# Loads of the attention heads issued from the SyncE queue in place of ScalarE's

## The chip, the cores and the metric

The kernel runs on one core of one Trainium2 chip. The metric is the device time of one launch in microseconds (us), the median of three runs; lower is better. Engines are named as in the profile: PE is the matrix engine, DVE the vector engine, ACT the scalar engine (ScalarE), POOL GpSimd, and SP the SyncE queue. A DMA is issued by an instruction in the program of SP or ACT, and the profile lists such issues as SPq and ACTq; the bytes then move on 16 DMA engines of the core.

## The reference, cut to what matters

One inference step of a trunk of two layers, in float32, on 640 tokens of width 1024: 512 noisy ("latent") tokens and 128 of a new prompt. In each layer one input projection feeds three groups of heads, whose outputs are put side by side for one output projection; a SwiGLU feed-forward part with a hidden width of 2816 follows, and both halves end in a layer norm with modulated shift, scale and gate.

```python
z = (x * (1 + scale_m) + shift_m) @ w_in          # columns split among A, B and C
o_a = diff_attention(q1, q2, k1, k2, v, lam)      # A: 4 heads, two softmax maps each
o_b, s_d = delta_mixer(...)                       # B: gated DeltaNet, both directions, chunks of 64
o_c, s_h = hgrn_mixer(...)                        # C: HGRN2, both directions, chunks of 16
o = concatenate([o_a, o_b, o_c])                  # then @ w_out, layer norm, feed-forward, layer norm

def diff_attention(...):                          # per block of 128 queries
    s1 = einsum(q1, k1) * scale;  s2 = einsum(q2, k2) * scale
    p = softmax(s1) - lam * softmax(s2)
    return einsum(p, v)
```

Latent queries read the 512 latent keys and 128 cached ones; the prompt's queries read the prompt's keys alone. New keys and values of the prompt, and the final states of B and C, are outputs too.

## The kernel before

Matrix products keep nearly full float32 accuracy by splitting an operand into a high part in the faster fp32r format and a remainder: for each weight tile `raw` that a DMA brings, ACT casts the high half of a tile `hl` (L273) and DVE subtracts to get the low half (L176). Tiles `hl` sit in a ring of four buffers, weight tiles `raw` in one that SP fills (L254).

A layer runs in stages that overlap. The input projection writes the queries and keys of all attention heads to scratch in DRAM (`qkhi` for the high parts, `qksc` for the low parts and the prompt, L1318 and L1319), values to `vsc`, and B's outputs to `osc`. Its last pieces are `ci`/`gt` (PE `pci`, one of five token blocks each) and `cq` (PE `pcq`, two blocks in two halves). Beside these runs the DeltaNet chain: PE steps `pdc`, and for each of five token blocks an output that goes through `do`, `doh` (one buffer) and a gate `gd` that SP loads, and is stored to `osc` by ACT (L1048). Then attention runs head after head beside HGRN (`ph`, `hq`, `hqm`) and the modulation products `psm`, whose weights `w_mod` SP loads.

The attention of a head needs 17 loads, which the change touches. `attn_load_qk` (L1139 to L1173) issues 12 into two buffers of the `hl` ring, the query tile `aqs` and the key tile `aks` (L1151 to L1157), and three of cached keys into `ack` (L1159, L1161), of which there is one buffer; PE then transposes (`pack`), and ACT and DVE put the result behind the latent keys (L1167, L1172). `attn_load` adds two loads of values into `avf` (L1183, L1184). Head 0's first 15 are called in `proj_C` ahead of the two `pcq` blocks (L1293), its values when attention begins (L1382), and those of head h+1 in the middle of head h (L1215). In attention PE computes scores `pas`, DVE their maximum `anm`, ACT the exponentials `ae` (L1131), PE transposes (`pat`, copied by ACT to `apT`) and multiplies by the values (`pao`, copied by ACT to `ao`, L1103).

The order of instructions on every engine is not that of the Python code: the program is built inside a context that simulates a timeline of all engines and places each instruction by it (`schedule_with_timeline_sim=True`, L1767). An engine then runs its own list strictly in that order, so an instruction that waits holds what stands behind it, DMA issues included. Completions of DMAs of both queues share eight semaphores that are taken in turn: a DMA is issued only when the eighth one before it has landed, whichever queue issued that.

Of the kernel before, what the change touches and what calls it, by code (L numbers as in the profile page):

```python
# [10 lines left out]
F32 = mybir.dt.float32  # L11
# [8 lines left out]
P = 128  # L20
D = 1024
DEPTH = 2
NLAT = 512
NPRO = 128
NTOK = NLAT + NPRO
NT = NTOK // P
# [83 lines left out]
def tile_trunk(  # L110
# [52 lines left out]
    def psS(cls, name):  # L163
        ps = ps_next(cls, [P, 512], name)
        return ps[:, 0, :] if len(ps.shape) == 3 else ps
# [4 lines left out]
    V, A, G, S = nc.vector, nc.scalar, nc.gpsimd, nc.sync  # L170
# [4 lines left out]
    def tt(eng, out, a, b, op):  # L175
        return eng.tensor_tensor(out, a, b, op)  # L176
# [276 lines left out]
    vsc = [dr.tile([NTOK, 512], F32, name=f"vsc{l}") for l in range(DEPTH)]  # L453
# [3 lines left out]
    qksc = [dr.tile([2, AH, P, NTOK], F32, name=f"qksc{l}") for l in range(DEPTH)]  # L457
    qkhi = [dr.tile([2, AH, P, NLAT], F32, name=f"qkhi{l}") for l in range(DEPTH)]
# [680 lines left out]
    def attn_load_qk(l, h, cls):  # L1139
        qs = phl.tile([P, 2, 1024], F32R, tag="hl", bufs=4, name="aqs")  # L1140
        ks = phl.tile([P, 2, 1024], F32R, tag="hl", bufs=4, name="aks")
        qd, qp = qs[:, 0].rearrange("p (m t) -> p m t", m=2), qs[:, 1, :P].bitcast(F32)
        kflat = ks.rearrange("p x t -> p (x t)")
        kd = kflat[:, :2 * NTOK].rearrange("p (m t) -> p m t", m=2)
        kl = [kflat[:, 2 * NTOK:3 * NTOK], qs[:, 1, P:P + NTOK]]
        kp = kflat[:, 3 * NTOK:].bitcast(F32)
        lo_ = qksc[l]
        qf_, kf_ = qd.bitcast(F32), kd.bitcast(F32)
        hv = [slice(64 * m, 64 * m + 64) for m in range(2)]
        for m in range(2):  # L1150
            A.dma_start(qf_[hv[m], m], qkhi[l][0, h, hv[m]])  # L1151
            A.dma_start(qf_[hv[1 - m], m], lo_[0, h, hv[m], :NLAT])
            A.dma_start(kf_[hv[m], :, :NLAT], qkhi[l][1, h].rearrange("(m j) t -> j m t", m=2))
            for i in range(2):
                A.dma_start(kl[m].bitcast(F32)[hv[i], :NLAT], lo_[1, h, hv[m], :NLAT])
        A.dma_start(qp, qksc[l][0, h, :, NLAT:])
        A.dma_start(kp, qksc[l][1, h, :, NLAT:])  # L1157
        ck = cp.tile([P, 2, P], F32, tag="ack", bufs=1, name=f"ack{l}_{h}")
        A.dma_start(ck[:, 0], cache_attn_k[0, l, :, h, :])  # L1159
        for m in range(2):  # L1160
            A.dma_start(ck[:, 1, hv[1 - m]], cache_attn_k[0, l, :, h, hv[m]])  # L1161
        ps = psS(cls, f"pack{l}_{h}")
        for m in range(2):
            nc.tensor.transpose(ps[:, m * P:(m + 1) * P], ck[:, m], ident)
        nc.tensor.transpose(ps[:, 2 * P:3 * P], kp, ident)
        ko = cp.tile([P, P], F32, tag="akp", bufs=1, name=f"akp{l}_{h}")
        A.copy(ko, ps[:, 2 * P:3 * P])  # L1167
        A.dma_start(new_attn_k[0, l, :, h, :], ko)
        for m in range(2):
            for i in range(2):  # L1170
                src = ps[hv[i], (i ^ m) * P:((i ^ m) + 1) * P]
                A.copy(kd[hv[i], m, NLAT:], src)  # L1172
                tt(V, kl[m][hv[i], NLAT:], src, kd[hv[i], m, NLAT:].bitcast(F32), ALU.subtract)  # L1173
        return qd, kd, kl, qp, kp
# [3 lines left out]
    def attn_load(l, h, ap_):  # L1178
        n_ = f"{l}_{h}"
        qd, kd, kl, qp, kp = early_qk.pop((l, h), None) or attn_load_qk(l, h, "pt")  # L1180
        vf = ap_.tile([P, NT + 1, P], F32, tag="avf", bufs=2, name=f"avf{n_}")
        hs = slice(h * P, (h + 1) * P)
        A.dma_start(vf[:, :NT], vsc[l][:, hs].rearrange("(t p) v -> p t v", p=P))  # L1183
        A.dma_start(vf[:, NT], cache_attn_v[0, l, :, h, :])  # L1184
        return qd, kd, kl, qp, kp, vf

    def attention(l, h, ap_, got):
        n_ = f"{l}_{h}"
        qd, kd, kl, qp, kp, vf = got.pop(h)
        for qt in range(LT):  # L1190
            nn = f"{n_}_{qt}"
            views = []
            qsl = slice(qt * P, (qt + 1) * P)
            for m in range(2):
                ps = psB("as", f"pas{nn}_{m}")
                for hf in range(2):
                    hsl = slice(hf * 320, (hf + 1) * 320)
                    mm(ps[:, hf, :320], qd[:, m, qsl], kd[:, m, hsl], start=True, stop=False)
                    mm(ps[:, hf, :320], qd[:, m, qsl], kl[m][:, hsl], start=False, stop=True)
                views.append(ps[:, :, :320])  # L1200
            p, ri = softmax_pair(l, views, NTOK, ap_, nn)
            pt = psS("pt", f"pat{nn}").rearrange("p (b t) -> p b t", t=P)
            po = psS("po", f"pao{nn}")
            for kt in range(LT):
                nc.tensor.transpose(pt[:, kt, :], p[:, kt * P:(kt + 1) * P], ident)
            nc.tensor.transpose(po[:, P:2 * P], p[:, LT * P:], ident)
            pT = ap_.tile([P, NT, P], F32, tag="apT", bufs=2, name=f"apT{nn}")
            A.copy(pT[:, :LT], pt)
            A.copy(pT[:, LT], po[:, P:2 * P])
            for kt in range(NT):  # L1210
                mm(po[:, :P], pT[:, kt, :], vf[:, kt if kt < LT else NT],
                   start=(kt == 0), stop=(kt == NT - 1))
            attn_tail(l, h, qt * P, po[:, :P], ri[:, 0:1], ap_, nn)
            if qt == PRE[l] and h + 1 < AH:
                got[h + 1] = attn_load(l, h + 1, ap_)  # L1215
            yield
# [57 lines left out]
    def proj_C(l, xT, wp):  # L1274
        W = w_in[l]
        for i in range(4):
            ps = gemm_T(colunit(W, C_CF + i * P), xT, f"pcf{l}_{i}")
            d_, a_ = i // 2, i % 2
            z = wp.tile([P, NTOK], F32, tag="cb", bufs=2, name=f"cf{l}_{i}")
            evac(z, ps, AF.Sigmoid)  # L1280
            V.tensor_scalar(z, z, lbi[:, l, d_, a_:a_ + 1], lbv[:, l, d_, a_:a_ + 1], ALU.mult, ALU.add)
            S.dma_start(cfs[l][i * P:(i + 1) * P, :], z)
            yield
        us = [(rowunit(W, 2 * i, 2, C_CI, 512), [2 * i, 2 * i + 1]) for i in range(4)]
        for tau in range(NT):
            ps = psS("n", f"pci{l}_{tau}")
            gemm_N(ps, 512, xT, tau, us)
            z = wp.tile([P, 256], F32, tag="ca", bufs=2, name=f"ci{l}_{tau}")
            A.copy(z, ps[:, :256])
            S.dma_start(cis[l][tau * P:(tau + 1) * P, :], z)  # L1290
            gate_out(l, ps[:, 256:512], prm[l]["cn"], tau, 256, wp)
            yield
        early_qk[(l, 0)] = attn_load_qk(l, 0, "d1")  # L1293
        for i in range(2):
            ps = gemm_T(colunit(W, C_CQ + i * P), xT, f"pcq{l}_{i}")
            z = wp.tile([P, NTOK], F32, tag="cb", bufs=2, name=f"cq{l}_{i}")
            evac(z, ps, AF.Silu)
            S.dma_start(cqs[l][i * P:(i + 1) * P, :], z)
            yield
# [45 lines left out]
    for l in range(DEPTH):  # L1345
# [35 lines left out]
        def attn():  # L1381
            got = {0: attn_load(l, 0, tp)}  # L1382
            for h in range(AH):
                yield from attention(l, h, tp, got)
            flush(l, 0)
# [182 lines left out]
        for tau in range(NT):  # L1568
# [4 lines left out]
            j = 0 if tau < LT else 1  # L1573
# [91 lines left out]
        for part, (f0, f1) in enumerate(FF_PARTS):  # L1665
# [39 lines left out]
            for nh, tau in order:  # L1705
                us = usn[nh] if nh in usn else usn.setdefault(nh, out_units(nh))
                cs = slice(nh * 512, (nh + 1) * 512)
                j = 0 if tau < LT else 1
# [62 lines left out]
```

## Time and profile before

| | |
|---|---|
| time, median of 3 runs | 2103.04 us (2100.37 to 2107.04) |
| the profiled execution: its time, its span | 2098.58 us, 2096.8 us |
| busy share PE, PE weight loads | 91%, 80% |
| busy share DVE, ACT, POOL | 69%, 38%, 43% |
| mean granted PE clock | 0.956 of full speed |
| bytes moved, mean rate | 249.36 MB, 119 GB/s |
| DMAs issued in the ACT program | 154: 136 loads of the heads, 10 stores of `osc`, 8 of new keys |

The span runs from the first instruction to the last; the time of that execution is 1.8 us longer. A share of busy time is a mean over unlike stages, so it is read together with the windows: a stage whose PE is busy all the time cannot be shortened by the other engines, a stage with idle PE time can.

### The profile page before, as it was taken

How to read it: one execution, taken by the hardware profiler on the slowest of the kernel's cores; microseconds unless marked ns; L12 is line 12 of the kernel's file. 1: busy time of each engine (PE TensorE's matmuls, PEld its weight loads, DVE VectorE, ACT ScalarE, POOL GpSimd, SP SyncE). 2: the span in 40 equal slices, each digit the busy share in tenths (PEclk: the TensorE clock that was granted, in tenths of full speed). 3: DMA queues.
4: the chain of work that ended last, by engine and by line, in shares of the span. 5: the costliest groups of instructions: out<-in, count | busy, mean ns of one | idle time of the engine just before them, and what ended most of it. 6: DMA issues, size and time to landing. Idle time of an engine off the chain costs nothing. (4 is left out here: it accounts for less than half of the span.)

```text
span 2096.8 us, 37785 instructions
## 1 busy us (share of the span) xinstructions
PE 1915.2 (91%) x14914; PEld 1681.5 (80%) x14914; DVE 1440.6 (69%) x2516; ACT 791.2 (38%) x1564; POOL 891.6 (43%) x988
## 2 busy tenths in 40 slices
PE   7999997778988999999989999977799799999996
PEld 5988986657768899989989979755687779989895
DVE  5458534778588866667666784368857897667676
ACT  3542322647143334333336323135742434334331
POOL 0375234766142132435156924357642411432445
PEclk7999998899999999999999999989889999999998
DMA  9423215872653322222434342377235232223221
GB/s 303 112 74 123 90 64 149 225 221 74 211 181 89 114 81 91 71 81 81 133 94 131 108 135 67 102 186 231 87 130 159 84 111 91 71 81 97 76 76 76
DMA packets 243399, 249.36 MB, mean 119 GB/s; under 512 B 19370, under 2 KB 190358, under 8 KB 243222
## 3 DMA queue, kind: packets, MB, share of 16 engines
q1 hardware_dynamic: 221046, 227.27, 35.0%
q10 hardware_dynamic: 22176, 19.67, 3.6%
q8 instruction: 118, 1.93, 0.4%
q14 instruction: 59, 0.48, 0.1%
HBM read 218.72 MB, written 28.18 MB: 118 GB/s over the span
## 5 line engine op out<-in xcount | busy, mean ns | idle before, releaser
L176 DVE TENSOR_TENSOR hl<-raw,hl 128x1024 fp32r<-128x1024 f32 (+1 forms) x210 | 280.1, 1337 | 88.7 <-ACT hl L273 70.9
L173 PE MATMUL pfo<-hl,ha 128*128 128x512 f32 x1320 | 312.9, 395 | 1.5 <-ACT hl L273 0.8
L173 PEld LDWEIGHTS pfo<-hl,ha 128*128 128x128 f32 x1320 | 246.1, 187 | 60.7 <-DVE ft L176 1.2
L176 POOL TENSOR_TENSOR r<-r,ft 128x512 f32<-128x512 f32 x96 | 143.0, 1510 | 248.4 <-DVE ft L176 247.7
L176 POOL TENSOR_TENSOR t<-raw 128x512 f32<-128x512 f32 x44 | 67.9, 1543 | 338.7 <-DMA raw<-in_w_ffn_in_dram 145.4
L173 PE MATMUL pfa<-xT,hl 128*128 128x320 f32 x1056 | 175.3, 316 | 8.7 <-DVE ms L176 3.5
L273 ACT CAST hl<-raw 128x1024 fp32r<-128x1024 f32 (+2 forms) x122 | 125.5, 1036 | 147.8 <-DMA raw<-in_w_ffn_out_dram 45.9
L173 PE MATMUL pfc<-sx,hl 128*128 128x320 f32 x1056 | 172.2, 311 | 9.4 <-ACT hl L1550 8.2
L173 PEld LDWEIGHTS pfa<-xT,hl 128*128 128x128 f32 x1056 | 162.7, 193 | 12.4 <-ACT sx L1513 3.9
L173 PEld LDWEIGHTS pfc<-sx,hl 128*128 128x128 f32 x1056 | 160.4, 189 | 13.0 <-ACT hl L1550 9.0
L1550 ACT CAST hl<-raw 128x1024 fp32r<-128x1024 f32 x88 | 92.1, 1051 | 207.7 <-PE pfo L173 104.4
L173 PE MATMUL paq<-xT,hl 128*128 128x320 f32 x768 | 123.1, 317 | 0.6 <-ACT az L1238 0.6
L173 PE MATMUL pop<-hl,xT 128*128 128x512 f32 x480 | 118.0, 402 | 0.7 <-ACT ae_p L1131 0.7
L173 PEld LDWEIGHTS paq<-xT,hl 128*128 128x128 f32 x768 | 115.7, 190 | 3.4 <-issue 1.2
L173 PEld LDWEIGHTS pop<-hl,xT 128*128 128x128 f32 x480 | 89.6, 191 | 24.9 <-issue 4.7
L176 POOL TENSOR_TENSOR hK<-hK,hT 64x256 f32<-64x256 f32 x120 | 90.6, 755 | 33.4 <-PE ph L173 27.7
L176 DVE TENSOR_TENSOR ft<-pfo,lg 128x512 f32<-128x512 f32 x96 | 63.8, 683 | 55.5 <-PE pfo L173 44.1
L173 PE MATMUL pfd<-xT,h 128*128 128x320 f32 x528 | 87.7, 316 | 9.9 <-DVE u L176 9.9
L176 DVE TENSOR_TENSOR t<-raw,t 128x512 f32<-128x512 f32 x88 | 73.9, 840 | 33.1 <-POOL t L176 33.0
L173 PE MATMUL pbq<-xT,hl 128*128 128x320 f32 x576 | 89.9, 313 | 1.0 <-DVE hl L176 0.4
L173 PEld LDWEIGHTS pfd<-xT,h 128*128 128x128 f32 x528 | 81.4, 193 | 11.4 <-issue 8.7
L173 PE MATMUL pfb<-sx,hl 128*128 128x320 f32 x528 | 88.6, 310 | 0.6 <-DVE hl L176 0.6
(409 smaller groups left out, 4213.0 us busy)
## 6 DMA issues: line engine op xcount, KB each, us to landing
raw<-in_w_ffn_in_dram SPq DMA_DIRECT2D x96, 512.0 KB
raw<-in_w_mod_dram SPq DMA_DIRECT2D x80, 512.0 KB
raw<-in_w_in_dram SPq DMA_DIRECT2D x56, 512.0 KB
raw<-in_w_ffn_out_dram SPq DMA_DIRECT2D x44, 512.0 KB
pc<-in_w_mod_dram SPq DMA_DIRECT2D x8, 1024.0 KB
raw<-in_w_out_dram SPq DMA_DIRECT2D x16, 512.0 KB
qksc<-az SPq DMA_DIRECT2D x16, 320.0 KB
qkhi<-azs SPq DMA_DIRECT2D x16, 256.0 KB
```

The source lines that it names most:

```text
L173: nc.tensor.matmul(out, lhsT, rhs, start=start, stop=stop, **kw)
L176: return eng.tensor_tensor(out, a, b, op)
L273: A.copy(hl[:, 0, :kt * n], raw[:, :kt * n])
L1550: A.copy(tile_[:, 0, :n], raw)
```

## The change

All 17 loads per head, 136 in the two layers, are issued by SP in place of ACT. Sizes, sources and targets stay as they are. The store of B's output to `osc` (L1048) and that of the new keys (L1168) stay on ACT.

```diff
         for m in range(2):
-            A.dma_start(qf_[hv[m], m], qkhi[l][0, h, hv[m]])
-            A.dma_start(qf_[hv[1 - m], m], lo_[0, h, hv[m], :NLAT])
-            A.dma_start(kf_[hv[m], :, :NLAT], qkhi[l][1, h].rearrange("(m j) t -> j m t", m=2))
+            S.dma_start(qf_[hv[m], m], qkhi[l][0, h, hv[m]])
+            S.dma_start(qf_[hv[1 - m], m], lo_[0, h, hv[m], :NLAT])
+            S.dma_start(kf_[hv[m], :, :NLAT], qkhi[l][1, h].rearrange("(m j) t -> j m t", m=2))
             for i in range(2):
-                A.dma_start(kl[m].bitcast(F32)[hv[i], :NLAT], lo_[1, h, hv[m], :NLAT])
-        A.dma_start(qp, qksc[l][0, h, :, NLAT:])
-        A.dma_start(kp, qksc[l][1, h, :, NLAT:])
+                S.dma_start(kl[m].bitcast(F32)[hv[i], :NLAT], lo_[1, h, hv[m], :NLAT])
+        S.dma_start(qp, qksc[l][0, h, :, NLAT:])
+        S.dma_start(kp, qksc[l][1, h, :, NLAT:])
         ck = cp.tile([P, 2, P], F32, tag="ack", bufs=1, name=f"ack{l}_{h}")
-        A.dma_start(ck[:, 0], cache_attn_k[0, l, :, h, :])
+        S.dma_start(ck[:, 0], cache_attn_k[0, l, :, h, :])
         for m in range(2):
-            A.dma_start(ck[:, 1, hv[1 - m]], cache_attn_k[0, l, :, h, hv[m]])
+            S.dma_start(ck[:, 1, hv[1 - m]], cache_attn_k[0, l, :, h, hv[m]])
...
-        A.dma_start(vf[:, :NT], vsc[l][:, hs].rearrange("(t p) v -> p t v", p=P))
-        A.dma_start(vf[:, NT], cache_attn_v[0, l, :, h, :])
+        S.dma_start(vf[:, :NT], vsc[l][:, hs].rearrange("(t p) v -> p t v", p=P))
+        S.dma_start(vf[:, NT], cache_attn_v[0, l, :, h, :])
```

Since the timeline decides the order, the lists of all five engines change in the mixer stages and a little in the start; ACT's shrinks from 1480 rows to 1356, SP's grows from 357 to 479. In the rows below a minus is a row of before, a plus one of after; names carry the layer and block number.

The first place is on ACT in layer 0, at the end of the projection, where head 0's loads stand: `hl` there are the halves of the weights for `pcq`.

```order
 L958 COPY dvn_4_2896<-pdt_4_2891 128x2x2x64
-L1153 DMA aks<-qkhi_443 64x2x512
-L1155 DMA aks<-qksc_441 64x512 x2
-L1048 DMA osc_429<-doh_1_2803 128x256
-L1153 DMA aks<-qkhi_443 64x2x512
-L1157 DMA aks<-qksc_441 128x128
+L273 CAST hl<-raw 128x1024
 L1289 COPY ci_4_3659<-pci_4_3634 128x256
 L1242 ACTIVATE gt_4_256_3662<-pci_4_3634 128x256
-L273 CAST hl<-raw 128x1024 x2
+L273 CAST hl<-raw 128x1024
+L1048 DMA osc_429<-doh_1_2803 128x256
```

The loads ahead of the casts are gone, and the store of block 1's output moved behind the casts.

The second place is ACT in layer 0 just ahead of the first exponential, whose table load is the last row; the rows with `cq_0` and `cq_1` are the last pieces of the projection.

```order
+L1048 DMA osc_429<-doh_3_3085 128x256
+L1238 ACTIVATE cq_0_3754<-pcq_0_0_1_3729 128x320
 L1238 ACTIVATE cq_1_3813<-pcq_1_0_0_3763 128x320
-L1161 DMA ack_1_3933<-in_cache_attn_k_dram 128x64
-L1172 CAST aks<-pack_0_3684 64x128
-L1048 DMA osc_429<-doh_3_3085 128x256
-L1172 CAST aks<-pack_0_3684 64x128
+L1048 DMA osc_429<-doh_4_3203 128x256
 L1238 ACTIVATE cq_1_3813<-pcq_1_0_1_3788 128x320
-L1183 DMA avf_0_3824<-vsc_433 128x5x128
-L1184 DMA avf_0_3824<-in_cache_attn_v_dram 128x128
 L1131 ACT_TABLE_LOAD
```

The loads left the list here too, but the stores of the last two B blocks (3 and 4) now stand ahead of the last `cq` pieces and so of the first exponential; before, that of block 4 came after the second exponential.

At the same place SP has these rows: the gate load `gd_4`, which block 4's output needs, and the loads of head 1.

```order
+L685 DMA gd_3_3094<-gsc_431 128x256
+L1159 DMA ack_1_3933<-in_cache_attn_k_dram 128x128
+L1161 DMA ack_1_3933<-in_cache_attn_k_dram 128x64 x2
+L1088 DMA out_dram<-dSf_999 64x2x64 x4
+L685 DMA gd_4_3212<-gsc_431 128x256
 L1298 DMA cqs_435<-cq_0_3754 128x640
-L685 DMA gd_3_3094<-gsc_431 128x256
-L685 DMA gd_4_3212<-gsc_431 128x256
-L1088 DMA out_dram<-dSf_999 64x2x64 x4
```

`gd_4` moved behind the `ack` loads of head 1, which need PE's `pack` of head 0, and behind the stores of the final state `dSf`.

The third place is ACT in layer 1, at the end of the projection.

```order
 L958 COPY dvn_4_13187<-pdt_4_13182 128x2x2x64
+L1048 DMA osc_430<-doh_1_13094 128x256
+L273 CAST hl<-raw 128x1024
 L1289 COPY ci_4_13950<-pci_4_13925 128x256
 L1242 ACTIVATE gt_4_256_13953<-pci_4_13925 128x256
 L273 CAST hl<-raw 128x1024
+L967 COPY du_10737<-pdu_4_13196 128x512
+L976 COPY dwT_10738<-pdw_4_13214 128x4x64 x2
 L1238 ACTIVATE cq_0_14045<-pcq_0_0_0_13995 128x320
-L976 COPY dwT_10738<-pdw_4_13214 128x4x64
-L1048 DMA osc_430<-doh_1_13094 128x256
```

Here the store of block 1's output moved ahead of the casts of the weights for `pcq`; before, it came after them and after the first `cq` piece.

## Rows read from the trace of the kernel before

**Rows 1.** The page: busy by engine; DMA queues (q1 SP's, q10 ACT's).

```profile
PE 1915.2 (91%) x14914; PEld 1681.5 (80%) x14914; DVE 1440.6 (69%) x2516; ACT 791.2 (38%) x1564; POOL 891.6 (43%) x988
...
q1 hardware_dynamic: 221046, 227.27, 35.0%
q10 hardware_dynamic: 22176, 19.67, 3.6%
```

**Rows 2.** Windows: stretch, length, busy us (instructions), granted clock, DMA share, GB/s.

```profile
700.00:1000.00 300.00, 298.24 (x1757) 276.14 (x1757) 214.12 (x304) 103.78 (x152) 112.26 (x72) 1.00 0.27 81
300.00:360.00 60.00, 47.76 (x606) 41.04 (x597) 25.57 (x74) 11.44 (x27) 25.38 (x34) 0.94 0.40 116
360.00:450.00 90.00, 68.65 (x738) 49.32 (x738) 66.67 (x145) 45.66 (x139) 61.14 (x107) 0.87 0.84 234
1360.00:1390.00 30.00, 19.24 (x169) 16.38 (x170) 16.55 (x46) 6.80 (x16) 14.29 (x23) 0.78 0.57 145
```

**Rows 3.** Tile `aks`, issues: count, ns min/median/max, first and last start.

```profile
L1155 ACTq DMA_DIRECT2D aks<-qksc x16: 452/582/1272, 316.2 to 1461.0; - x16
```

**Rows 4.** The same for tile `ack`.

```profile
L1161 ACTq DMA_DIRECT2D ack<-in_cache_attn_k_dram x16: 334/360/452, 1.1 to 1471.6; - x16
```

**Rows 5.** Timeline of ACT, layer 0: start, duration, line, what, [idle before, releaser].

```profile
310.18 0.52 ACTq L1151 DMA_DIRECT2D aqs<-qkhi  x1
...
320.93 0.35 ACTq L1048 DMA_DIRECT2D osc<-doh  x1
...
321.97 0.69 ACTq L1157 DMA_DIRECT2D aks<-qksc  x1
...
323.25 1.99 ACT L273 CAST hl<-raw 128x1024 fp32r<-128x1024 f32 x2
```

**Rows 6.** Timeline of PE: its longer waits in both layers.

```profile
324.35 0.85 PE L173 MATMUL pcq<-xT,hl 128*128 128x320 f32 x4 [2.46 <-ACT hl L273]
327.33 3.04 PE L173 MATMUL pcq<-xT,hl 128*128 128x320 f32 x10 [2.14 <-DVE hl L176]
...
359.17 1.41 PE L173 MATMUL pas<-aks,aqs 128*128 128x320 f32 x5 [4.52 <-ACT ae L1131]
...
368.59 1.44 PE L173 MATMUL pas<-aks,aqs 128*128 128x320 f32 x4 [2.97 <-ACT ae L1131]
...
1382.03 1.44 PE L173 MATMUL pas<-aks,aqs 128*128 128x320 f32 x4 [5.13 <-ACT ae L1131]
```

**Rows 7.** Timeline of ACT, layer 0, around the first exponential.

```profile
345.03 0.35 ACTq L1048 DMA_DIRECT2D osc<-doh  x1
...
352.83 0.35 ACTq L1048 DMA_DIRECT2D osc<-doh  x1
...
355.85 1.28 ACT L1131 ACT_TABLE_LOAD   x1 [1.60 <-DMA osc<-doh]
358.23 0.79 ACT L1131 ACTIVATE ae<-pas,anm 128x640 f32<-128x640 f32 x1 [1.10 <-DVE anm L1125]
...
360.32 0.33 ACTq L1048 DMA_DIRECT2D osc<-doh  x1
...
367.16 0.59 ACT L1208 COPY apT<-pat 128x512 f32<-128x512 f32 x1 [3.03 <-DMA aks<-qkhi]
```

**Rows 8.** Timeline of ACT, layer 1.

```profile
1343.18 1.04 ACT L273 CAST hl<-raw 128x1024 fp32r<-128x1024 f32 x1 [8.31 <-DMA aks<-qksc]
...
1354.71 0.35 ACTq L1048 DMA_DIRECT2D osc<-doh  x1
...
1375.72 0.35 ACTq L1048 DMA_DIRECT2D osc<-doh  x1
...
1381.09 0.79 ACT L1131 ACTIVATE ae<-pas,anm 128x640 f32<-128x640 f32 x1 [1.31 <-DVE anm L1125]
```

**Rows 9.** Waits, 300 to 545 us: engine line, releaser, us, times, longest.

```profile
DVE doh L176 <- DMA osc<-doh: 11.6, 3, 7.1
...
PE psm L173 <- DMA raw<-in_w_mod_dram: 8.6, 9, 2.2
```

## The prediction

> **What bounds the kernel now.** I read the page first, then windows, then the waits of PE, then the ACT timeline around them. The page says that PE is busy 91% of the span and ACT 38%; SP's queue q1 carries 221046 packets, ACT's q10 22176 [rows 1]. A mean hides where the slack is, so the windows come next. In a stretch of the feed-forward part PE is busy 298.24 of 300 us: nothing that ACT or a DMA queue does shortens that. In the mixer stages it is not: 47.76 of 60, then 68.65 of 90 in layer 0, and 19.24 of 30 where layer 1's attention begins [rows 2]. That is 12.2, 21.4 and 10.8 us of idle PE. The change acts only there (and a little in the start), and because the PE-bound feed-forward part follows each stage, a microsecond won or lost in a stage goes on to the end.
>
> The reader should then see what PE waits for there: the casts of weights on ACT and DVE (2.46 and 2.14 us), the first exponential of layer 0 (4.52), one a little later (2.97), and the first of layer 1 (5.13) [rows 6]. The question is which of these ACT is late for because of its DMA issues.
>
> **What the change takes from ACT.** An issue takes 0.582 us in the median for a query or key piece [rows 3] and 0.360 for a small one [rows 4]. With 96 of the first kind and 40 of the second, 55.9 + 14.4 is about 70 us of ACT's program (an estimate). Issues aren't counted as busy, which is why ACT looks idle at 38%. Only those in front of awaited work count:
>
> Casts in layer 0. ACT issues head 0's twelve loads from 310.18 to 322.66, and a store of `osc` in their midst at 320.93 holds the last of them; the casts that PE awaits start at 323.25 [rows 5]. Without the loads, and with that store behind the casts, they are free to run when their weights have landed. PE's two waits, 4.60 us together, go [rows 6]; I take 4.0, since PE will meet some other operand.
>
> First exponential of layer 0. The loads that stood before it go as well, yet I count nothing for it. The last query pieces now stand behind the stores of blocks 3 and 4, and these come from a chain with one `doh` buffer: issues at 345.03, 352.83 and 360.32, 7.5 to 7.8 us apart, so each next block waits for a store to land (DVE waits 11.6 us for that in three goes) [rows 7, 9]. If the chain starts 4 us earlier with the casts, block 4's store is issued at 356.3; its issue of 0.33 and the table load of 1.28 bring that to 357.9, and a copy comes between: about 358.2, where the exponential starts now [rows 7]. From below: if this chain were not in the way the 4.52 us would go; from above: if it doesn't move, the distance of 5.40 from block 3's store to the exponential applies to block 4's, and the exponential comes at 365.7, 7.5 late. I take the middle, 0.
>
> The wait of 2.97 us at 368.59 is behind a copy of `apT` that ACT starts at 367.16, 3.03 late, because the value load of head 1 ahead of it waited for an earlier load to land [rows 6, 7]. That load is on SP afterwards: I take 3.0.
>
> Heads 1 to 3 of both layers. Loads stand between exponentials and copies of the running head, but here the DMA engines are busy 0.84 of the time at 234 GB/s [rows 2]. Moving the issue moves no bytes. I take 1.5 us in all, between 0 and 6.
>
> A rule bears on this. The Trainium skill ("DMA: Bandwidth & Descriptors", Issuing engines are not separate DMA queues) says that DMAs of all issuing engines end up on the same 16 DMA engines, and that spreading the issue over engines saves only the sequencer's time, usually little beside the transfer. The busy share of 0.84 agrees for bytes [rows 2]; the 12.5 us of one run of issues shows that the sequencer's time need not be little for what is queued behind it [rows 5]. By the rule alone the sum would be about 0, which is the second rival below.
>
> Layer 1. Twelve loads in a row hold a cast back to 1343.18, 8.31 us, but PE has other work then. The first exponential is at 1381.09, behind block 3's store at 1375.72 [rows 8]: the same chain. The loads of values and of head 1 between the two are gone; of PE's 5.13 us [rows 6] I take 1.5.
>
> **What it adds.** In layer 1 block 1's store now stands ahead of the casts for `pcq`. It was issued at 1354.71, the casts began at 1343.18 [rows 8], so they can come up to 11.5 us later; PE loses `pcq` as cover while it waits for the chain. That work then fills waits further on, where 10.8 of 30 us are idle [rows 2]. From both sides: 0 (all refilled, or the chain faster) to 8; I take 2.0.
>
> On SP the loads go to the queue that carries weights. Each issue that waits for a buffer or for PE now holds weights behind it, and the reverse: `gd_4` behind the loads of `ack`, `w_mod` behind head 2's and 3's loads. PE already waits 8.6 us for `w_mod` in nine goes in layer 0 [rows 9]. An issue costs SP what it cost ACT at most; a doubling of these waits would be 8.6, none is 0, and fewer (`w_mod` waited on the shared semaphores before too) could give 2 back. I take 1.0, near none, since the order puts several `w_mod` loads ahead of head 3's.
>
> In the start three loads of `ack` leave ACT's list and enter SP's behind weights; head 0 needs them 300 us later: 0, within 2 either way, as the start is reordered a little on all engines.
>
> **Sum.** -4.0 + 0 - 3.0 - 1.5 - 1.5 + 2.0 + 1.0 = -7.0 us. The profiled execution took 2098.58 us (its span is 2096.8), so 2091.6 on its basis; it lies 4.5 below the median of the runs, 2103.04, on which I forecast 2096.0. Its own range: the gains full with no price (-4.6 - 4.5 - 3 - 4 - 3, about -19) at one end, no gain at the other: 2084 to 2103.
>
> **Rivals.**
>
> Slower: stores in front of awaited work. The chain of `osc` doesn't start earlier, and what ACT now does behind its stores waits: the first exponential of layer 0 by 7.5, the `pcq` casts of layer 1 by 4 in effect, SP's mixing 1. Against it only the 4.0 of the casts stand: +8.5, 2111.5. For it: the order rows on ACT in both layers, and the regular 7.5 us of the chain [rows 7]. Against: the chain shares ACT with the loads before, and loses them. It decides from the point where block 4's store is issued later than about 356.5.
>
> No change. Transfers, not issues, set these stages; by the rule above too. What ACT wins it waits again for bytes or for the chain: -3 to +3, 2103. For: 0.84 busy DMA engines and the wait that a chain ends at each first exponential [rows 2, 7, 8]. Against: the casts of layer 0, where the waiting is on issues with DMA at 0.40 [rows 2].
>
> A larger gain. All five waits of PE go, 17.2 us [rows 6], and heads 1 to 3 give 6: -23, 2080. The windows with much idle PE have a lower granted clock (0.87 and 0.78 of 2.4 GHz, a mix of its two levels, against 1.00 in the feed-forward part [rows 2]); fewer gaps could raise it. For: the order was made anew with ACT free. Against: the chain of stores.
>
> That the change doesn't do what it says can be left out: the order shows all loads on SP.
>
> **How the numbers follow.** Differences below 0.3%, 6.3 us, can't be told from none here. Forecast 0.45 (0.32 of it faster by more, 0.13 within); slower rival 0.24; no change 0.18 (0.13 within, 0.02 faster, 0.03 slower); larger gain 0.13. So faster 0.47, same 0.26, slower 0.27. The range for 8 in 10 cuts the far ends of both outer cases: 2077 to 2113.
>
> **What would show it.** The casts of layer 0 by 319 or earlier and no PE wait above 1 us ahead of `pcq` there; the first exponential of layer 0 at 356 to 361, with block 4's store just ahead of it; no wait of an `apT` copy for a key load; in layer 1 the casts later than now and yet the first exponential within 3 us of 1381 less what was won before; PE's waits for `w_mod` between 6 and 12 us in layer 0. I am wrong if the first exponential of layer 0 starts beyond 363 or before 353, or if the feed-forward parts differ in length by more than 2 us: nothing here reaches them.

## The result, and the profile after

The changed kernel takes 2094.8 us in the median of nine runs (2090.42 to 2101.12); the kernel before, beside it, 2103.67. The ratio is 0.9949, with a 95% interval of 0.9931 to 0.9968: about 10.7 us less by the ratio (6.7 to 14.5), 8.9 by the medians. The forecast was 7.0 less. The profiled execution took 2094.80 us with a span of 2093.0, only 3.8 less than the one of before, which lies 5 us under its median; so the traces tell where, and the ratios how much.

First the page and windows of the kernel after, with the same columns as before [rows 1, 2].

```profile
PE 1912.6 (91%) x14914; PEld 1676.2 (80%) x14914; DVE 1439.1 (69%) x2516; ACT 792.7 (38%) x1564; POOL 883.5 (42%) x988
...
q1 hardware_dynamic: 240630, 245.11, 38.4%
...
q10 hardware_dynamic: 2592, 1.84, 0.3%
```

```profile
700.00:1000.00 300.00, 298.98 (x1777) 278.17 (x1776) 210.93 (x303) 104.44 (x153) 111.50 (x72) 1.00 0.28 83
300.00:360.00 60.00, 49.97 (x618) 42.98 (x617) 28.69 (x80) 13.10 (x31) 29.48 (x43) 0.90 0.43 118
360.00:450.00 90.00, 71.66 (x831) 53.27 (x830) 77.59 (x163) 51.69 (x158) 67.72 (x114) 0.88 0.77 214
1360.00:1390.00 30.00, 19.86 (x180) 17.84 (x180) 19.56 (x49) 10.91 (x26) 15.20 (x25) 0.87 0.66 161
```

The loads have changed queue, 19584 packets from q10 to q1. PE does more in the same windows of the mixer stages: 831 matrix instructions from 360 to 450 us in place of 738. The feed-forward part is as full as it was. And the DMA engines, which I had taken to set the stage of the running heads, are less busy there than before: 0.77 against 0.84 [rows 2]. One window could only mean that bytes moved later, so here is the whole stretch of the heads, from the first score to the first product of the output projection, layer 0 and layer 1, first before, then after:

```profile
353.30:531.00 177.70, 140.60 (x1468) 109.37 (x1466) 140.79 (x311) 105.06 (x314) 116.71 (x191) 0.89 0.61 177
1373.90:1557.60 183.70, 141.72 (x1406) 111.23 (x1404) 144.17 (x318) 108.03 (x321) 118.82 (x195) 0.86 0.52 147
```

```profile
350.70:524.40 173.70, 140.21 (x1469) 107.96 (x1468) 142.46 (x307) 105.83 (x312) 116.56 (x192) 0.88 0.70 207
1372.70:1551.10 178.40, 138.24 (x1409) 107.29 (x1407) 142.54 (x313) 107.25 (x319) 116.73 (x193) 0.88 0.54 152
```

The same matrix instructions, give or take three, take 4.0 and 5.3 us less, and more bytes a second move meanwhile, 207 GB/s for 177 in layer 0. The DMA engines had not been the limit of this stage.

The timeline of ACT in layer 0 around the casts and the first exponential, to be held against [rows 5, 7]:

```profile
315.54 1.05 ACT L273 CAST hl<-raw 128x1024 fp32r<-128x1024 f32 x1 [1.11 <-PE pci L173]
...
317.45 1.05 ACT L273 CAST hl<-raw 128x1024 fp32r<-128x1024 f32 x1
...
346.25 0.34 ACTq L1048 DMA_DIRECT2D osc<-doh  x1
...
352.40 0.33 ACTq L1048 DMA_DIRECT2D osc<-doh  x1
352.77 0.44 ACT L1238 ACTIVATE cq<-pcq 128x320 f32<-128x320 f32 x1 [5.38 <-POOL doh L176]
353.23 1.28 ACT L1131 ACT_TABLE_LOAD   x1
354.52 0.79 ACT L1131 ACTIVATE ae<-pas,anm 128x640 f32<-128x640 f32 x1
```

The casts start 7.7 us earlier and PE's two waits ahead of `pcq` are gone. The last query piece does stand behind block 4's store, and waits 5.38 us for POOL's `doh` there, but that store is 7.9 us earlier than before (352.40 against 360.32), more than the 4 I had allowed, so the exponential comes at 354.52 and not at 358.2.

In layer 1 the same engine, against [rows 8]:

```profile
1345.58 0.36 ACTq L1048 DMA_DIRECT2D osc<-doh  x1
1345.98 1.05 ACT L273 CAST hl<-raw 128x1024 fp32r<-128x1024 f32 x1 [7.25 <-PE pdu L173]
...
1372.61 0.33 ACTq L1048 DMA_DIRECT2D osc<-doh  x1
...
1375.71 0.79 ACT L1131 ACTIVATE ae<-pas,anm 128x640 f32<-128x640 f32 x1 [0.99 <-DVE anm L1125]
```

The casts are later, by 2.8 us, although block 1's store ahead of them is 9.1 earlier than it was. The first exponential is 5.4 us earlier, but layer 1's projection had begun 7.0 earlier (the first product of `paq`, the queries of attention, at 1127.4 for 1134.4). From the last product of `paq` to the first score it is 166.0 us, 162.8 before: this part of layer 1 got longer, not shorter.

What PE waits for in the whole run, first before, then after (engine and line, releaser, us in total, times, longest):

```profile
PE pas L173 <- ACT ae L1131: 24.2, 20, 5.1
...
PE psm L173 <- DMA raw<-in_w_mod_dram: 12.9, 14, 2.2
```

```profile
PE pas L173 <- ACT ae L1131: 12.3, 15, 3.4
...
PE psm L173 <- DMA raw<-in_w_mod_dram: 9.9, 7, 4.4
...
PE pao L173 <- DMA avf<-vsc: 9.3, 2, 4.7
```

Scores wait for exponentials half as long, the waits for `w_mod` fell a little, and a new wait is there: the first product with the values waits for head 0's `avf`, twice, 9.3 us together. Of ACT itself, before, the waits on DMAs from 353 to 531 us were these:

```profile
ACT ao L1103 <- DMA aqs<-qksc: 6.2, 1, 6.2
...
ACT ao L1103 <- DMA hq<-cqs: 3.2, 1, 3.2
...
ACT apT L1208 <- DMA aks<-qkhi: 3.0, 1, 3.0
...
ACT ajk L1104 <- DMA hv<-cis: 2.2, 1, 2.2
```

A copy of a result does not need `aqs`, `hq` or `hv`. It stood behind an issue that waited until an earlier DMA had landed, of either queue. After, no exponential and no copy of ACT in the attention of either layer waits for a DMA; only casts wait for their weights.

### The profile page after: what moved, and what is told of

The parts are those of the page before. It is cut to its first block, busy times and chain, and to the rows that moved or that the text cites. A ratio compares the mean times of both kernels' runs of the same rounds, so it can differ in the third digit from the quotient of the medians.

```text
span 2093.0 us, 37831 instructions
## 1 busy us (share of the span) xinstructions
PE 1912.6 (91%) x14914; PEld 1676.2 (80%) x14914; DVE 1439.1 (69%) x2516; ACT 792.7 (38%) x1564; POOL 883.5 (42%) x988
## 4 chain that ended last, share of the span: by engine, by line
PE 26%; DVE 10%; POOL 5%; DMA 3%; issue 3%; ACT 2%; SPq 1%; POOLq 0%; ACTq 0%; DVEq 0%
PE pfo L173 6%; PE pfd L173 3%; PE pfc L173 3%; PE pfa L173 3%; PE pop L173 3%; PE pfb L173 1%; PE pci L173 1%; DVE hl L176 1%; DVE hq L176 1%; PE pcf L173 1%; POOL r L176 1%; PE pbq L173 1%; PE ph L173 1%; DVE fs L176 1%; DMA avf<-vsc 1%
## 5 line engine op out<-in xcount | busy, mean ns | idle before, releaser
L173 PEld LDWEIGHTS pfc<-sx,hl 128*128 128x128 f32 x1056 | 161.5, 190 | 13.5 <-ACT hl L1550 7.8
L173 PE MATMUL pop<-hl,xT 128*128 128x512 f32 x480 | 122.4, 407 | 0.0
```

Source lines behind the costliest of these rows:

```text
L173: nc.tensor.matmul(out, lhsT, rhs, start=start, stop=stop, **kw)
```

## Experiments

The theory from the forecast: ACT is late because issues stand ahead of awaited work, above all at the casts and at the copy behind head 1's values, nearly all of it in layer 0. Its rivals: the time is won inside the running heads of both layers; or a new order of the lists moves the time by itself. Each kernel was timed in five rounds beside the kernel before; in the expectations of e1 to e4 a minus is against the kernel before.

**By layer and by head.** One line chooses the queue:

```diff
-            S.dma_start(...)            # all 17 loads
+            Q.dma_start(...)            # Q = S if l == 0 else A    (e1)
+                                        # Q = S if l == 1 else A    (e2)
+                                        # Q = S if h == 0 else A    (e3)
+                                        # Q = S if h > 0 else A     (e4)
```

> Only layer 0's 68 loads on SP, layer 1's stay on ACT. Theory (issues in front of awaited work, sized as forecast): layer 0 carries nearly all, -7 us, time about 2096. Rival (time is won in the attention heads of both layers alike, since the stretch from the first scores to the output projection fell by 4.0 and 5.3 us in the profiles): half, -4 to -5. Rival (only the order of the lists matters): anything from -5 to +5, not adding up with the kernel that moves layer 1 alone.

> Only layer 1's 68 loads on SP. Theory: 0 (within 2 us). Rival of both layers alike: -4 to -5. Rival of order: anything, and the two parts do not add up to the -9 of the whole change.

> Only head 0's loads of both layers on SP (34 of 136). Theory: the casts of layer 0 (-4) and the first exponentials (-1 to -2): -5. Rival of the heads: -1 or none, since heads 1 to 3 stay on ACT. Rival of order: anything, no sum.

> Only the loads of heads 1 to 3 of both layers on SP (102 of 136). Theory: the copy that waited for head 1's values (-3) and the rest of the heads (-1.5), SP's price +1: -3.5. Rival of the heads: -8, nearly the whole change. Rival of order: anything, no sum.

| | moved to SP | median us | ratio to before (95%) | us by the ratio |
|---|---|---|---|---|
| e1 | layer 0 | 2097.41 | 0.9963 (0.9948 to 0.9978) | -7.8 |
| e2 | layer 1 | 2098.08 | 0.9966 (0.9950 to 0.9982) | -7.2 |
| e3 | head 0 | 2102.23 | 0.9987 (0.9969 to 1.0005) | -2.7 |
| e4 | heads 1 to 3 | 2092.82 | 0.9933 (0.9910 to 0.9955) | -14.1 |

(The last column is the ratio less one, times before's median beside it, 2105.14.) Both layers give about the same, against the theory. Head 0, where the theory had the casts and the first exponentials, gives nothing that can be told from noise, though the theory's -5 is still inside its interval (-6.5 to +1.1). Heads 1 to 3 give 14.1 (9.5 to 18.9) where the theory had 3.5. The rival of the heads holds, and its -8 was too small. The trace of e4 places the gain, in the same two stretches as above:

```profile
355.50:526.70 171.20, 137.36 (x1469) 108.28 (x1468) 142.12 (x311) 105.64 (x312) 120.15 (x193) 0.91 0.62 180
1374.40:1548.80 174.40, 139.61 (x1409) 109.37 (x1407) 145.25 (x317) 108.03 (x321) 117.95 (x194) 0.86 0.55 155
```

They are 6.5 and 9.3 us shorter than before, while the first exponentials start where they did (358.10 and 1381.17 us, 358.23 and 1381.09 before). Of the 15.8 us, 10.5 are idle time of PE; the other 5.3 are in the time that PE was busy with the same instructions, at a granted clock of 0.91 for 0.89 in layer 0 and 0.86 in both in layer 1. This is one trace of each kernel: that of e2 shows layer 1's stretch no shorter (184.9 us), though its runs are 7.2 faster.

The lines of PE's waits say the same; here e3, then e4:

```profile
PE pas L173 <- ACT ae L1131: 21.8, 15, 5.8
```

```profile
PE pas L173 <- ACT ae L1131: 13.9, 14, 4.4
```

With head 0 moved the scores still wait 21.8 us for exponentials, against 24.2 before; with the others moved 13.9.

**Which loads of heads 1 to 3.** In e5 only the values, in e6 only the twelve query and key loads:

```diff
-        S.dma_start(vf[...], ...)
+        (S if h > 0 else A).dma_start(vf[...], ...)     # e5, all others on A
...
-            S.dma_start(qf_[...], ...)                  # and the other 11
+            (S if h > 0 else A).dma_start(qf_[...], ...)  # e6, ack and avf on A
```

> Only the value loads of heads 1 to 3 of both layers on SP (12 loads), all others on ACT. Theory I (the time of issuing on ACT between exponentials): 12 issues of 0.38 us are a tenth of the 51 us that heads 1 to 3 took, so -1 of the -12 measured for all of them. Theory W (ACT held by loads that wait for an earlier DMA to land; 15.3 us of ACT waits on DMAs in the heads of layer 0 and 8.5 in layer 1 before): the value load is one of the places, -3 to -4. Order alone: anything within 4 either way.

> Only the 12 query and key loads of heads 1 to 3 on SP (72 loads), ack and values stay on ACT. Theory I: 72 x 0.58 = 42 of 51 us of issues, -10. Theory W: -5 to -8, since the ACT waits behind aqs and aks loads go and those behind the value loads stay.

Measured: e5 2098.67, ratio 0.9972 (0.9962 to 0.9983), -5.9 us (-8.0 to -3.6). e6 2085.23, ratio 0.9918 (0.9899 to 0.9936), -17.3 (-21.2 to -13.5), the fastest kernel of the case; its interval and that of the changed kernel (0.9931 to 0.9968) overlap only at their ends. The values gain more than the 1 us that their share of the issues would; the 3 to 4 of the theory of waits (W) touch the interval, but the trace of e5 does not bear that theory out: in the attention of the two layers ACT waits 16.0 and 12.6 us for DMAs, against 16.9 and 8.5 before. The query and key loads carry the most, more than either theory said. In e6 the values of all heads and `ack` are still on ACT, and ACT waits there again for DMAs (6.1 and 6.3 us; `ao` and `ae` behind `hq`, 2.1 and 1.8 us in layer 1), yet the wait of PE for `avf` is absent. So neither the time of issuing (I) nor these waits alone give the gains in their sizes; how the gain divides between them is open. The waits of PE in e6:

```profile
PE pas L173 <- ACT ae L1131: 16.2, 14, 5.2
...
PE psm L173 <- DMA raw<-in_w_mod_dram: 10.4, 9, 2.7
```

**More issues, same bytes.** Each query and key load cut in two by partitions, on ACT (e7) and on SP (e8), 96 more in all:

```diff
-            A.dma_start(qf_[hv[m], m], qkhi[l][0, h, hv[m]])
+            for z in (0, 32):
+                A.dma_start(qf_[64 * m + z:64 * m + z + 32, m], qkhi[l][0, h, 64 * m + z:64 * m + z + 32])
...              # likewise the others; e8 with S
```

> All loads on ACT as before, each query and key load cut in two by partitions: 96 more issues, same bytes and rows. Theory I: ACT spends some 40 to 56 us more on issues, and the loss is about the gain of the change over again, +8 to +12. Theory W: more loads in flight on the shared semaphores, +3 to +12 too; if neither holds (order alone), within 3 of before.

> All loads on SP as after, each query and key load cut in two: 96 more issues on SP. If the gain comes from ACT being free, this stays within 3 us of the changed kernel (about 2095 to 2098), since SP's time isn't awaited. If SP's queue, now with everything in it, is near its limit, +6 or more.

Measured: e7 2137.7, ratio 1.0159 (1.0144 to 1.0174), +33.4 against before. e8 2108.79, ratio 1.0029 (1.0014 to 1.0043), +6.1 against before and so some 17 against the changed kernel. The issues of e7 and their length, as in [rows 3]:

```profile
L1154 ACTq DMA_DIRECT2D aqs<-qkhi x32: 308/366/1550, 311.4 to 1501.7; - x32
L1155 ACTq DMA_DIRECT2D aqs<-qksc x32: 308/434/1536, 311.8 to 1502.0; - x32
```

A half takes 0.43 us to issue in the median where a whole took 0.60. Summed over the traces, ACT issues query and key loads for 88.1 us in e7 and for 56.1 before, 32 us more, and the kernel loses 33; SP issues for 87.2 us in e8 and for 57.4 in the changed kernel, and 17 are lost. So each load more cost about 0.35 us of the kernel's time on ACT, 0.17 on SP. The first fits the theory that issuing on ACT is on the path, but does not show it alone: in layer 1's attention ACT's waits for DMAs grew too, from 8.5 to 29.4 us, and the granted clock was 0.943 in the mean of e7's runs, 0.954 in those of before beside them. The second says that SP's time is not free either, or that twice as many loads cost something on any queue; no run tells which. The part of the expectation by which e8 stays within 3 us failed.

**Order alone.** All loads on ACT, written with the keys ahead of the queries, which makes the timeline place everything anew:

```diff
+            A.dma_start(kf_[hv[m], :, :NLAT], ...)     # and kl, ahead of
             A.dma_start(qf_[hv[m], m], ...)
             A.dma_start(qf_[hv[1 - m], m], ...)
-            A.dma_start(kf_[hv[m], :, :NLAT], ...)
```

> A control for the order of the lists: all loads on ACT as before, only written with a head's key loads ahead of its query loads, so that the timeline places everything anew. If the effect of a new order by itself is small, within 4 us of before (2100 to 2108). If order alone carries the results so far, a change of 8 or more either way.

Measured: 2104.16, ratio 0.9991 (0.9976 to 1.0006). This new order moves the time by less than can be told, though the first exponential of layer 0 comes at 352.31, 5.9 us earlier than before. It is one order, not a bound for all; but the results above are not simply that.

**Fewer loads.** On top of e6, the low half of a key, loaded twice to two groups of 64 partitions, in one DMA:

```diff
-            for i in range(2):
-                Q.dma_start(kl[m].bitcast(F32)[hv[i], :NLAT], lo_[1, h, hv[m], :NLAT])
+            Q.dma_start(kl[m].bitcast(F32)[:, :NLAT], bc(lo_[1, h, hv[m], :NLAT], 0, 2))
```

> The kernel with the query and key loads of heads 1 to 3 on SP, and in all heads the two loads that put the same low key half into two groups of partitions made one (16 DMAs fewer, same bytes written). If what a load costs is its issue and its place among the loads in flight (cutting 96 loads in two cost 17 us on SP and 33 on ACT, 0.17 and 0.35 each), -3 to -6 against the kernel without the merge: about 2080. If the bytes set it: no change, 2085.

Measured: 2160.54, ratio 1.0252 (1.0221 to 1.0283), some 70 us slower than e6. The expectation was wrong in sign. The issue of the merged load itself is short (L1155), but the one behind it is not (L1156), and weights come late. Of the issues, those on SP:

```profile
L1155 SPq DMA_DIRECT2D aqs<-qksc x6: 523/542/568, 349.6 to 1514.7; - x6
L1156 SPq DMA_DIRECT2D aqs<-qksc x6: 464/2396/3952, 350.2 to 1515.3; - x6
```

```profile
PE psm L173 <- DMA raw<-in_w_mod_dram: 39.8, 11, 8.7
```

L1156 here is the load of the prompt's queries that follows; its issue takes 2.4 us in the median, where it took 0.57 before. PE's waits for `w_mod` rise from 10.4 to 39.8 us. The semaphores of the trace show more. Every other query and key load counts 16 updates until it has landed; each of the 16 merged loads has three, one about 1 us after its issue and the last, on SP, 14.3 us after it in the median for `aqs` and 9.8 for `aks`. The two loads in its place in e6 had landed after 3.7. The load behind it (L1156) lands after 13.9 us, 3.3 in e6. What followed was late with it. Three updates in place of 16 suggest that the merged load moved over few of the 16 DMA engines; that is an inference, and whether the source read twice or the shape of the access brings it about is not settled, as no run splits it otherwise.

**Stores on SP too.** The changed kernel with L1048 on SP:

```diff
-        A.dma_start(osc[l][tau * P:(tau + 1) * P, :], head_norm_out(...))
+        S.dma_start(osc[l][tau * P:(tau + 1) * P, :], head_norm_out(...))
```

> The changed kernel (all loads on SP) with the ten stores of osc on SP too. The forecast put the first exponentials behind these stores on ACT. If they bound there, the first exponential of each layer comes 2 to 5 us earlier and the time falls by 3 to 8 (2087 to 2092). If the heads after it set the time (rival), within 3 us of 2095; if SP's queue is crowded, slower than that.

Measured: 2095.52, ratio 0.9950 (0.9933 to 0.9968), the same as the changed kernel. In layer 0 the first exponential starts at 354.07 in place of 354.52:

```profile
354.07 0.79 ACT L1131 ACTIVATE ae<-pas,anm 128x640 f32<-128x640 f32 x1
```

So the stores on ACT hold it by no more than that. In layer 1 it starts at 1379.81, 4.1 us later than in the changed kernel, and the time is the same: the place of the first exponentials isn't what the time hangs on, as e4 and e9 say too. The waits of PE moved, for exponentials from 12.3 to 8.6 us, for `avf` from 9.3 to 11.2.

**Head 0's values back on ACT.** This was to remove the new wait of 9.3 us:

```diff
-        S.dma_start(vf[:, :NT], ...)
+        (A if h == 0 else S).dma_start(vf[:, :NT], ...)   # and vf[:, NT]
```

> The changed kernel with only the value loads of head 0 (two per layer) back on ACT. In the changed kernel PE's first product with the values waits 4.73 us in layer 0 and 4.60 in layer 1 for them, since SP issues them behind the loads of head 1's queries and of HGRN's gates; where head 0's values stay on ACT (heads 1 to 3 alone moved) there is no such wait. If that is what the whole change loses against the kernels with a part of it: both waits gone or under 1 us, -5 to -9 against the changed kernel, 2086 to 2090. If other waits take the place, within 3 us of 2095.

Measured: 2098.74, ratio 0.9969 (0.9957 to 0.9982), not faster than the changed kernel, if anything slower. The wait for `avf` is gone, and others have grown:

```profile
PE psm L173 <- DMA raw<-in_w_mod_dram: 18.7, 15, 2.3
PE pas L173 <- ACT ae L1131: 14.9, 14, 5.8
```

The wait for `w_mod` went from 9.9 to 18.7 us, that for exponentials from 12.3 to 14.9: 11.4 us in place of 9.3. A wait that is seen is not yet what would be won without it.

## Why the prediction was right, and where it was not

The direction, the size in sum (7.0 forecast, 10.7 with 6.7 to 14.5 measured) and the reason that ACT was late because of the loads were right. How the sum was shared out was not, and that it came near is in part luck: a term that was too small stood beside a price that was too small.

- Casts of layer 0 (4.0): in the trace they come 7.7 us earlier and PE's 4.60 us of waits go, as forecast. In time, head 0's loads as a whole, casts and first exponentials together, gave 2.7 with an interval from 6.5 gained to 1.1 lost (e3), so the 4.0 is neither borne out nor excluded. In the traces the first score of layer 0 is 2.6 us earlier than before, not 7.7 (350.75, 353.31): most was waited for again by then.
- First exponential of layer 0 (0): it came at 354.52, ahead of the 356 to 361 that I named, with block 4's store just before it. The chain of stores ran nearly 8 us earlier, not 4. The rival of stores in front of awaited work is refuted in layer 0 by that: the exponential came 3.7 us earlier, not 7.5 later. Moving the stores off ACT (e11) changed the time by nothing that can be told.
- Values of head 1 in layer 0 (3.0): the wait of the `apT` copy is gone, as forecast, and so is PE's of 2.97 behind it; the values of heads 1 to 3 in both layers gave 5.9 (e5). No run moves that one load alone.
- Heads 1 to 3 of both layers (1.5, "between 0 and 6"): the step that failed. With head 1's values added it was 4.5 for what measured 14.1 (e4; 9.5 to 18.9). I let the busy share of 0.84 stand for a limit by bytes. It was not: after the change the whole stretch of layer 0's heads is 4.0 us shorter at 207 GB/s for 177, and in e4 the two stretches together are 15.8 us shorter. ACT's list is one in which exponentials, copies and loads alternate, and each load takes time to issue and could be held by a DMA of any queue that had not landed; which of the two costs more stays open. The rule quoted from the Trainium skill ("DMA: Bandwidth & Descriptors", Issuing engines are not separate DMA queues) would have made it 0. What it states of bytes is not contradicted by any run; but what it counts as saved, the sequencer's time, was not small for the work behind it here: 72 loads moved gave 17.3 us (e6).
- Layer 1 (-1.5 for the exponential, +2.0 for the casts behind the store): layer 1 alone gave 7.2 (e2), not about 0. The price is about what it cost: from the last product of `paq` to the first score the traces have 166.0 and 165.4 us where layer 1's loads were moved (after, e2), 162.8 and 163.1 where not (before, e1), though e9, with nothing moved, has 165.0. What I missed is layer 1's share of the heads.
- SP's mixing (+1.0): probably too small. 96 more issues on SP cost 17 us (e8), and heads 1 to 3 alone gain 14.1 where all heads gain 10.7. If so, the whole change holds a price that its part does not show, and the too small +1.0 and the too small gain happened to cancel. PE's waits for `w_mod` in layer 0 (300 to 545 us) are no part of it: 5.3 us in place of 8.6, below the 6 to 12 that I named. Where that price sits is open: the visible wait for head 0's values was taken away (e12) and nothing was won. The intervals of e4 and of the whole change overlap, so the difference may be noise; e6 stands further off.

The kernel with only the queries and keys of heads 1 to 3 on SP (e6, 2085.23) beats both kernels. It was timed in one set of runs. The rival of a larger gain had a higher clock for one of its reasons: the mean granted clock is 0.956 in both profiled executions, so these two traces show no gain by it. Neither of the signs of being wrong came: the first exponential of layer 0 lies between 353 and 363, and the feed-forward parts, from the first `pfa` to the last `pfd`, took 434.3 and 430.8 us for 436.1 and 430.4 before.

## What to carry to other kernels

An engine that computes and also issues loads is late not by its busy share but by what stands in its list ahead of awaited work: count the issues between two awaited instructions, and the waits of copies on DMAs they have no use for. A high DMA share in one window does not make bytes the limit of a stage: here the same work went through at a higher rate once the engines were less held up. The other queue isn't free: move the loads that stand among awaited work, leave those that hurt no one, and time the parts, since they need not add up.

## What was not expected of the hardware

Cutting a load in two shortens its issue by little more than a quarter, to 0.43 us in the median from 0.60, and each of 96 more cost about 0.35 us of the kernel's time on ACT, 0.17 on SP (e7, e8). And one load in place of two can be far dearer: a DMA that reads 64 rows twice into 128 partitions landed 14.3 us after its issue in the median (`aqs`, on SP) in place of 3.7, the next issue on its queue took 2.4 us in the median, up to 3.95, and with 16 such loads the kernel was 70 us slower (e10).
